# Seven quarter products in three sweeps instead of two, in the second MLP product of a decoder block

## The chip, the core and the metric

The kernel runs on one core of a Trainium2 chip. The engines are named as in the profile: PE (TensorE, matrix products; PEld is its weight load), DVE (VectorE), ACT (ScalarE), POOL (GpSimd) and SP (SyncE, which here only issues DMAs). PE writes to PSUM, which has 8 banks of 128 x 512 float32; all else works in SBUF, and data come from and go to DRAM by DMA. The metric is the device time of one execution in microseconds (us): 830.0 us, the median of three runs (829.31, 830.0 and 831.16).

## What is computed

One decoder layer on 512 tokens of width 1024 in float32: a mixer (attention, a gated convolution, a gated sum and a projection), then an MLP with 4096 features. The change touches the MLP's second product and what follows it:

```python
def squared_relu_mlp(h, w_ff1, w_ff2):
    return jnp.square(jax.nn.relu(h @ w_ff1)) @ w_ff2
...
f = squared_relu_mlp(rms_norm(x, norm_mlp_pre), w_ff1, w_ff2)
x = x + rms_norm(f, norm_mlp_post)
```

## The kernel before

**Split products.** Float32 accuracy is kept by writing each operand as a high part and a low part (`split`, L725: ACT casts the high part, DVE subtracts to get the low one), and by three matmuls for each product: high x high, high x low, low x high (`mm3`, L84 to 88). A matmul has 128 x 128 weights and moves 512 columns.

**First MLP product.** `h @ w_ff1` is done in 32 blocks j of 128 features. `wsplit` (L99) loads a block's weights in two pieces of 256 KB into buffers of tag raw (6 of them, L47), splits them into tags whi and wlo (4 each, L48), and `ff1_part` (L685) does 24 matmuls of 512 tokens into one PSUM bank. `ff1_end` (L694) squares the rectified result (ACT, then DVE at L699) into f1[j // 2]: a tile per pair p of blocks, holding features of both blocks (rows 0 and 1) for both token halves. The tiles of pairs 0 to 13 take all 14 buffers of tag w, the last two come from tag ra.

**Second MLP product as seven quarter products.** For a pair p, `f @ w_ff2` is a 2 x 2 block product: A has two token halves (256 tokens) and two feature rows, B two feature rows and two halves of 512 output columns. The Winograd form of Strassen's method replaces eight block products with seven, at the price of sums and differences of the quarters, which DVE forms. A block product is 6 matmuls (two token tiles x three), and its two banks accumulate over all 16 pairs.

- The first sweep is interleaved with the first product: after the blocks of pair p, `first_operands(p)` (L737) loads four quarters of w_ff2 (`quarter`, L720, tag raw), forms s23 and t3, t2, t4, and splits them; `first_sweep(p - 1)` (L757) issues the three block products of the pair before: P7 = s3 t3, P6 = s2 t2, P4 = a22 t4.
- The second sweep (L802 to 816) goes over the 16 pairs again. `second_operands(p)` (L762) loads the four quarters anew, forms t1, splits the f tile and the four right operands; `second_products` (L779) issues P1, P5, P2 and P3. The operands of pair 0 and product P1 of pair 0 stand ahead of the last first sweep.
- Between them (L807 to 812) e, g and h take up the sums of the first sweep, which frees its banks.
- The end (L834 to 854) does the products of the last two pairs (TAIL, L54) token tile by token tile. As each bank is complete, DVE combines it into o_, the output tiles. `post(t)` (L827) takes the squares' sums (ACT, and two small operations on POOL, L649 and L145), multiplies by the gain (L831), and `finish` (L820) scales, adds the residual x1 and stores (L824, L825). Token tiles t + 2 (lower half) and t (upper half) are finished in the same pass, t = 0 and then 1.

**What sets the order.** Each engine, and SP's queue of DMAs, works through its instructions in order. The order is not that of the source alone: a scheduler deals out instructions as their operands and buffers come free in its own model, earlier source lines first. A tile of a tag takes a buffer only when an earlier tile of that tag has been read for the last time. PSUM tags: ps (3 banks), sc (2), cv (2), tp (1). In the second MLP product further tags matter: h (hpool, 4 buffers; first-sweep operands, then the f tile's splits) and sw (r3, 4 buffers; right operands of the later sweeps).

Of the kernel before, what the change touches and what calls it, by code (L numbers as in the profile page):

```python
# [19 lines left out]
P = 128  # L20
# [38 lines left out]
def decoder_block(ctx: ExitStack, tc: tile.TileContext, a: dict, out: bass.AP):  # L59
# [676 lines left out]

    def first_operands(p):  # L737
# [17 lines left out]
        return (s3, s2, [a22[:, h] for h in half]), w  # L755
# [6 lines left out]
    def second_operands(p):  # L762

        b12, b11, b21, b22 = (quarter(2 * p + r, c, *t) for r, c, *t in (
            (0, 1, "whi", NSPLIT), (0, 0), (1, 0), (1, 1)))
        t1 = stage.tile([P, 512], F32, tag="wlo", name=f"t1{p}", bufs=NSPLIT)
        l = htile(f"l{p}")
        w = [r3.tile([P, 4, 512], F32R, tag="sw", name=f"y{x}{p}", bufs=4) for x in "hl"]
        split(l[:, 0:2, :], l[:, 2:4, :], f1[p])
        split(w[0][:, 0, :], w[1][:, 0, :], b11)  # L770
        dve.tensor_tensor(t1, b12, b11, ALU.subtract)
        for n, src in ((1, t1), (2, b21), (3, b22)):
            split(w[0][:, n, :], w[1][:, n, :], src)
        return l, w


    LEFT = ((0, 0), (0, 1), (1, 0), (1, 1))

    def second_products(p, ops, which, toks=(0, 1)):  # L779
        l, w = ops  # L780
        for n in which:
            r, c = LEFT[n]
            products(bcc[n], [l[:, r, half[c]], l[:, 2 + r, half[c]]], [x[:, n, :] for x in w], p == 0, p == NP - 1, toks)

    ops = {}
    for p in range(NP):
# [10 lines left out]
        if p == 1:  # L797
            acc = [[scs(f"p70"), scs("p71")], [cvtile("p60"), cvtile("p61")], [tps("p40"), ps("p41")]]
# [3 lines left out]
    second = second_operands(0)  # L802
    bcc = [[ps(f"p1{t}") for t in range(2)]]
    second_products(0, second, (0,))
    first_sweep(NP - 1, ops.pop(NP - 1))

    e, g = (ratile(n) for n in ("e", "g"))  # L807
    h = wtile("h")
    for t in range(2):
        act.copy(e[:, t, :], acc[1][t])  # L810
        dve.tensor_tensor(g[:, t, :], acc[0][t], e[:, t, :], ALU.add)
        dve.tensor_tensor(h[:, t, :], g[:, t, :], acc[2][t], ALU.subtract)
    bcc += [[cvtile(f"p5{t}") for t in range(2)], [scs(f"p2{t}") for t in range(2)], [tps("p30"), ps("p31")]]
    second_products(0, second, (1, 2, 3))
    for p in range(1, NP - TAIL):
        second_products(p, second_operands(p), range(4))
# [3 lines left out]
    def finish(t, r):  # L820
        for c, n in ((0, 512), (512, 512)) if t != 1 else ((0, 512), (512, 256), (768, 256)):
# [3 lines left out]
            sp.dma_start(out[t * P:(t + 1) * P, c:c + n], piece)  # L825

    def post(t):  # L827
        src = [o_[t][:, hf, :] for hf in range(2)]
        r = square_sums(src, f"o{t}")
        for hf in range(2):  # L830
            dve.tensor_tensor(src[hf], src[hf], gout[:, hf * 512:(hf + 1) * 512], ALU.mult)  # L831
        finish(t, r)

    last = [(p, second_operands(p)) for p in range(NP - TAIL, NP)]  # L834
    for t in range(2):
        v = stile(f"v{t}")
        for n in (0, 1, 2, 3):
            for p, x in last:
                second_products(p, x, (n,), (t,))
            bank = bcc[n][t]  # L840
            if n == 0:
                act.copy(v, bank)
                dve.tensor_tensor(o_[t + 2][:, 0, :], v, h[:, t, :], ALU.add)
            elif n == 1:
                dve.tensor_tensor(g[:, t, :], g[:, t, :], bank, ALU.add)
                dve.tensor_tensor(e[:, t, :], e[:, t, :], bank, ALU.add)  # L846
                dve.tensor_tensor(o_[t + 2][:, 1, :], g[:, t, :], v, ALU.add)
                post(t + 2)
                pool.tensor_tensor(e[:, t, :], e[:, t, :], v, ALU.add)  # L849
            elif n == 2:  # L850
                dve.tensor_tensor(o_[t][:, 0, :], v, bank, ALU.add)
            else:
                dve.tensor_tensor(o_[t][:, 1, :], e[:, t, :], bank, ALU.add)
                post(t)
# [61 lines left out]
```

## Time and profile before

| | us |
|---|---|
| median of three runs | 830.0 |
| the profiled execution | 830.19 |
| its span, first to last instruction | 828.4 |
| PE busy | 797.4 (96%) |
| DVE busy | 633.0 (76%) |
| ACT busy | 419.7 (51%) |
| POOL busy | 215.6 (26%) |

The table and all rows below are of the profiled execution. Times in rows count from the start of its span. A matmul's recorded duration is longer than the distance from one to the next, as matmuls are pipelined, so rates are read from starts. The granted PE clock is given as a share of full speed. An idle time in brackets ends with what released the engine; SPq marks DMA issues of SP, and a row that ends in "x2" merges two instructions.

### The profile page before, as it was taken

How to read it: one execution, taken by the hardware profiler on the slowest of the kernel's cores; microseconds unless marked ns; L12 is line 12 of the kernel's file. 1: busy time of each engine (PE TensorE's matmuls, PEld its weight loads, DVE VectorE, ACT ScalarE, POOL GpSimd, SP SyncE). 2: the span in 40 equal slices, each digit the busy share in tenths (PEclk: the TensorE clock that was granted, in tenths of full speed). 3: DMA queues.
4: the chain of work that ended last, by engine and by line, in shares of the span. 5: the costliest groups of instructions: out<-in, count | busy, mean ns of one | idle time of the engine just before them, and what ended most of it. 6: DMA issues, size and time to landing. Idle time of an engine off the chain costs nothing. (4 is left out here: it accounts for less than half of the span.)

```text
span 828.4 us, 11002 instructions
## 1 busy us (share of the span) xinstructions
PE 797.4 (96%) x3786; PEld 660.7 (80%) x3786; DVE 633.0 (76%) x1046; ACT 419.7 (51%) x792; POOL 215.6 (26%) x203
## 2 busy tenths in 40 slices
PE   8989999999999999899999999999999999999992
PEld 8967888888888887687878898888888888788871
DVE  5689999999999996596573547857657657798777
ACT  6667775867673233365442324434334334555642
POOL 3244433433434645648711100000000000000003
PEclk9999999999999999999999999999999999999997
DMA  8412121122112223245450014544434334466422
GB/s 265 137 41 90 52 80 51 53 80 70 68 62 100 91 101 104 89 162 188 159 191 1 27 49 155 178 135 144 141 127 153 128 127 165 154 210 202 157 67 101
DMA packets 54344, 96.36 MB, mean 116 GB/s; under 512 B 6288, under 2 KB 11280, under 8 KB 54288
## 3 DMA queue, kind: packets, MB, share of 16 engines
q1 hardware_dynamic: 53856, 94.09, 34.1%
q0 software_dynamic: 432, 1.57, 0.5%
q8 instruction: 30, 0.49, 0.3%
q14 instruction: 26, 0.21, 0.1%
HBM read 93.54 MB, written 2.10 MB: 115 GB/s over the span
## 5 line engine op out<-in xcount | busy, mean ns | idle before, releaser
L559 DVE SCALAR_TENSOR_TENSOR cv<-u,convw,cv 128x512 f32<-128x512 f32 x232 | 161.9, 747 | 0.2
L87 PE MATMUL pf<-h2l,whi_f 128*128 128x512 f32 (+1 forms) x256 | 97.4, 380 | 0.0
L86 PE MATMUL pf<-h2h,whi_f 128*128 128x512 f32 (+1 forms) x256 | 97.3, 380 | 0.0
L88 PE MATMUL pf<-h2h,wlo_f 128*128 128x512 f32 (+1 forms) x256 | 97.3, 381 | 0.0
L112 DVE TENSOR_TENSOR wlo_f<-raw_f,whi_f 128x512 fp32r<-128x512 f32 x60 | 41.1, 690 | 65.1 <-ACT whi_f L111 63.9
L849 POOL TENSOR_TENSOR e<-e,v 128x512 f32<-128x512 f32 x2 | 3.2, 1600 | 329.4 <-DVE e L846 329.4
L111 ACT CAST whi_f<-raw_f 128x512 fp32r<-128x512 f32 x60 | 36.9, 621 | 85.0 <-PE pf L87 50.0
L112 POOL TENSOR_TENSOR wlo_gt<-raw_gt,whi_gt 128x512 fp32r<-128x512 f32 x32 | 43.9, 1374 | 50.1 <-ACT whi_gt L111 50.1
L87 PEld LDWEIGHTS pf<-h2l,whi_f 128*128 128x128 f32 x256 | 48.2, 188 | 9.9
L86 PEld LDWEIGHTS pf<-h2h,whi_f 128*128 128x128 f32 x256 | 48.2, 188 | 9.9
L88 PEld LDWEIGHTS pf<-h2h,wlo_f 128*128 128x128 f32 x256 | 48.2, 188 | 9.8
L86 PE MATMUL pg<-hTh,whi_gt 128*128 128x512 f32 x128 | 51.4, 402 | 0.0
L88 PE MATMUL pg<-hTh,wlo_gt 128*128 128x512 f32 x128 | 50.6, 396 | 0.0
L87 PE MATMUL pg<-hTl,whi_gt 128*128 128x512 f32 x128 | 50.5, 395 | 0.0
L86 PE MATMUL p<-yh,l 128*128 128x512 f32 x128 | 50.4, 395 | 0.0
L87 PE MATMUL p<-yl,l 128*128 128x512 f32 x128 | 50.4, 395 | 0.0
L88 PE MATMUL p<-yh,l 128*128 128x512 f32 x128 | 50.2, 395 | 0.0
L726 ACT CAST yh<-f 128x512 fp32r<-128x512 f32 x48 | 28.0, 617 | 36.8 <-PE p L87 27.6
L727 DVE TENSOR_TENSOR yl<-f,yh 128x512 fp32r<-128x512 f32 x48 | 31.7, 687 | 14.8 <-ACT yh L726 14.7
L111 ACT CAST whi_gt<-raw_gt 128x512 fp32r<-128x512 f32 x32 | 19.8, 618 | 40.1 <-PE pg L87 37.0
L726 ACT CAST xh<-t 128x512 fp32r<-128x512 f32 x48 | 29.6, 619 | 19.5 <-DVE t L751 19.5
L727 DVE TENSOR_TENSOR xl<-t,xh 128x512 fp32r<-128x512 f32 x48 | 31.5, 684 | 0.5 <-ACT xh L726 0.5
(314 smaller groups left out, 2278.6 us busy)
## 6 DMA issues: line engine op xcount, KB each, us to landing
f<-in_w_ff SPq DMA_DIRECT2D x128, 256.0 KB, 3.0
raw_f<-in_w_ff SPq DMA_DIRECT2D x64, 256.0 KB, 3.0
raw_gt<-in_w_zm SPq DMA_DIRECT2D x32, 256.0 KB, 2.5
raw_gb<-in_w_zm SPq DMA_DIRECT2D x16, 256.0 KB, 2.6
raw_ga<-in_w_zm SPq DMA_DIRECT2D x16, 256.0 KB, 2.6
raw_wo<-in_w_o SPq DMA_DIRECT2D x16, 256.0 KB, 2.6
raw_pw<-in_w_pw SPq DMA_DIRECT2D x16, 256.0 KB, 2.7
raw_wout<-in_w_out SPq DMA_DIRECT2D x16, 256.0 KB, 2.7
```

The costliest lines, as they stand in the source:

```text
L86: pe.matmul(o, lhsT=lh, rhs=rh, start=first, stop=False)
L87: pe.matmul(o, lhsT=lh, rhs=rl, start=False, stop=False)
L88: return pe.matmul(o, lhsT=ll, rhs=rh, start=False, stop=last)
L111: recent[act] = act.copy(hi, raw)
L112: recent[e] = e.tensor_tensor(lo, raw, f32(hi), ALU.subtract)
L559: dve.scalar_tensor_tensor(co[j] if tap == CW - 1 else acc[j], src, convw[:, i, tap:tap + 1], acc[j], ALU.mult, ALU.add)
L726: act.copy(hi, src)
L727: dve.tensor_tensor(lo, src, f32(hi), ALU.subtract)
L849: pool.tensor_tensor(e[:, t, :], e[:, t, :], v, ALU.add)
```

## The change

The same seven products are dealt out as three, two and two. The first sweep now takes P1 = a11 b11, P6 = s2 t2 and P7 = s3 t3. In it DVE also forms t1 and t4, in the raw buffers of b12 and b21, and SP writes both to DRAM (`keep`, 2 x 256 KB per pair). The second sweep takes P5 and P4, for which t1 and t4 are read back (`later_operands(p, 0)`, two loads); with them the lower token half (tiles 2 and 3) is complete. The third sweep takes P2 and P3 with two quarters of w_ff2 (`later_operands(p, 1)`). During its first 14 pairs the generator `lower()` forms and finishes tiles 2 and 3, a step per pair. The last two pairs are again done tile by tile, now for tiles 0 and 1 only. The operands of pairs 0 and 1 of the second sweep, and P5 of both, stand ahead of the last first sweep. Matmuls per pair: 42, as before. Loads per pair: 8 quarter-sized DMAs, as before, and two writes.

```diff
+    dram = open_pool(ctx, "dram", bass.MemoryType.DRAM)
+    def keep(name, p, src):
+        kept[name, p] = dram.tile([P, 512], F32, tag=f"{name}{p}", name=f"{name}{p}")
+        sp.dma_start(kept[name, p], src)
     def first_operands(p):
...
-        a22 = stile(f"a22{p}", F32R)
-        split(a22[:, half[0]], a22[:, half[1]], f[:, 1, half[1]])
+        a11 = stile(f"a11{p}", F32R)
+        split(a11[:, half[0]], a11[:, half[1]], f[:, 0, half[0]])
+        split(w[0][:, 0, :], w[1][:, 0, :], b11)
...
-        ts = [stile(f"t{n}{p}") for n in (3, 2, 4)]
-        for n, (t, x, y, op) in enumerate(((ts[0], b22, b12, ALU.subtract), (ts[1], ts[0], b11, ALU.add), (ts[2], ts[1], b21, ALU.subtract))):
-            dve.tensor_tensor(t, x, y, op)
-            split(w[0][:, n, :], w[1][:, n, :], t)
-        dve.tensor_tensor(f[:, 1, half[1]], f[:, 1, half[0]], s23[:, half[0]], ALU.subtract)
+        t3, t2 = (stile(f"t{n}{p}") for n in (3, 2))
+        dve.tensor_tensor(t3, b22, b12, ALU.subtract)
+        dve.tensor_tensor(t2, t3, b11, ALU.add)
+        split(w[0][:, 2, :], w[1][:, 2, :], t3)
+        split(w[0][:, 1, :], w[1][:, 1, :], t2)
+        dve.tensor_tensor(b12, b12, b11, ALU.subtract)
+        keep("t1", p, b12)
+        dve.tensor_tensor(b21, t2, b21, ALU.subtract)
+        keep("t4", p, b21)
+        dve.tensor_tensor(f[:, 0, half[0]], f[:, 1, half[0]], s23[:, half[0]], ALU.subtract)
...
-    def second_operands(p):
-        b12, b11, b21, b22 = (quarter(2 * p + r, c, *t) for r, c, *t in (
-            (0, 1, "whi", NSPLIT), (0, 0), (1, 0), (1, 1)))
...
+    def later_operands(p, beta):
+        if beta:
+            raw = [quarter(2 * p + 1, c) for c in range(2)]
+        else:
+            raw = []
+            for n, (tag, bufs) in (("t1", ("whi", NSPLIT)), ("t4", ("raw", NRAW))):
+                raw.append(stage.tile([P, 512], F32, tag=tag, name=f"{n}b{p}", bufs=bufs))
+                sp.dma_start(raw[-1], kept[n, p])
+        l = hpool.tile([P, 4, 2 * P], F32R, tag="h", name=f"l{beta}{p}", bufs=4)
+        w = r3.tile([P, 4, 512], F32R, tag="sw", name=f"y{beta}{p}", bufs=4)
+        split(l[:, 0:2, :], l[:, 2:4, :], f1[p][:, :, half[1 - beta]])
+        for n in range(2):
+            split(w[:, n, :], w[:, 2 + n, :], raw[n])
         return l, w
...
-    e, g = (ratile(n) for n in ("e", "g"))
-    h = wtile("h")
+    u1, u2 = (ratile(n) for n in ("u1", "u2"))
+    u3 = wtile("u3")
     for t in range(2):
+        act.copy(u1[:, t, :], acc[0][t])
+    for t in range(2):
+        dve.tensor_tensor(u2[:, t, :], acc[1][t], u1[:, t, :], ALU.add)
+        dve.tensor_tensor(u3[:, t, :], acc[2][t], u2[:, t, :], ALU.add)
...
+    def lower():
+        for t in range(2):
+            yield from post(t + 2, (
+                lambda: dve.tensor_tensor(o_[t + 2][:, 0, :], u3[:, t, :], bcc[1][t], ALU.subtract),
+                lambda: dve.tensor_tensor(o_[t + 2][:, 1, :], u3[:, t, :], bcc[0][t], ALU.add),
+                lambda: dve.tensor_tensor(u2[:, t, :], u2[:, t, :], bcc[0][t], ALU.add)))
+    rest = lower()
+    for p in range(NP - TAIL):
+        later_products(p, 1, later_operands(p, 1))
+        next(rest, None)
+    last = [(p, later_operands(p, 1)) for p in range(NP - TAIL, NP)]
...
     for t in range(2):
-        v = stile(f"v{t}")
-        for n in (0, 1, 2, 3):
+        for n, src in ((0, u1), (1, u2)):
             for p, x in last:
-                second_products(p, x, (n,), (t,))
...
+                later_products(p, 1, x, (n,), (t,))
+            dve.tensor_tensor(o_[t][:, n, :], src[:, t, :], bcc[2 + n][t], ALU.add)
+        for _ in post(t, ()):
+            pass
```

`post` is now a generator: it does the combinations it is given, then what `post` and `finish` did, and yields after each DVE step (7 steps for a lower tile).

## Rows read from the trace of the kernel before

**Rows 1.** The page: busy time of each engine, share of the span.
```profile
PE 797.4 (96%) x3786; PEld 660.7 (80%) x3786; DVE 633.0 (76%) x1046; ACT 419.7 (51%) x792; POOL 215.6 (26%) x203
```

**Rows 2.** By stretch: length; busy of PE, PEld, DVE, ACT, POOL; clock; DMA; GB/s.
```profile
501.64:711.93 210.29, 210.29 (x910) 170.96 (x909) 138.48 (x253) 85.85 (x153) 0.00 (x0) 1.00 0.43 146
711.93:723.68 11.75, 9.77 (x43) 7.66 (x42) 10.19 (x18) 8.28 (x15) 0.00 (x0) 1.00 0.47 159
723.68:812.10 88.42, 88.42 (x379) 70.61 (x377) 73.44 (x104) 48.45 (x81) 3.02 (x4) 1.00 0.47 156
812.10:828.40 16.30, 0.00 (x0) 0.00 (x0) 11.57 (x18) 3.05 (x9) 5.18 (x7) 0.63 0.27 97
...
720.00:760.00 40.00, 40.00 (x173) 32.26 (x172) 36.95 (x52) 24.05 (x38) 0.00 (x0) 1.00 0.57 188
```

**Rows 3.** Timeline at the change of sweeps: start, duration, engine, line, operation.
```profile
711.53 0.40 PE L88 MATMUL pf<-h2h,wlo_f 128*128 128x512 f32 x1
715.65 0.40 PE L88 MATMUL p<-xh,a 128*128 128x512 f32 x1
718.03 0.73 PE L86 MATMUL p<-xh 128*128 128x512 f32 x2 [1.98 <-ACT xh L726]
...
708.95 0.62 ACT L726 CAST yh<-f 128x512 fp32r<-128x512 f32 x1 [1.96 <-PE pf L87]
712.02 0.60 ACT L696 ACTIVATE rl<-pf 128x512 f32<-128x512 f32 x1 [1.41 <-PE pf L88]
715.80 0.62 ACT L726 CAST yh<-f 128x512 fp32r<-128x512 f32 x1 [1.72 <-DMA f<-in_w_ff]
...
712.65 0.69 DVE L699 TENSOR_TENSOR f<-pf,rl 128x512 f32<-128x512 f32 x1 [1.15 <-ACT rl L696]
715.47 0.42 DVE L747 TENSOR_TENSOR s<-f 128x256 f32<-128x256 f32 x1
```

**Rows 4.** Timeline of the end, by engine.
```profile
811.70 0.40 PE L88 MATMUL p<-yh,l 128*128 128x512 f32 x1
...
803.71 0.69 DVE L843 TENSOR_TENSOR o<-v,h 128x512 f32<-128x512 f32 x1
806.11 1.79 DVE L831 TENSOR_TENSOR o<-o,g_out 128x512 f32<-128x512 f32 x1
820.62 0.67 DVE L853 TENSOR_TENSOR o<-e,p 128x512 f32<-128x512 f32 x1
823.67 1.54 DVE L824 SCALAR_TENSOR_TENSOR o<-o,r_o,x 128x512 f32<-128x512 f32 x3 [0.85 <-POOL r_o L145]
...
821.38 0.63 ACT L647 ACTIVATE j_o<-o 128x512 bf16<-128x512 f32 x1 [1.80 <-DVE o L853]
...
822.20 0.79 POOL L649 TENSOR_SCALAR v_o<-ss_o 128x1 f32<-128x1 f32 x1 [3.22 <-ACT j_o L647]
```

**Rows 5.** One pair of the first sweep: timeline, and its groups (idle last).
```profile
651.94 0.68 DVE L699 TENSOR_TENSOR f<-pf,rl 128x512 f32<-128x512 f32 x1
659.84 0.69 DVE L112 TENSOR_TENSOR wlo_f<-raw_f,whi_f 128x512 fp32r<-128x512 f32 x1 [1.32 <-ACT whi_f L111]
667.21 0.69 DVE L699 TENSOR_TENSOR f<-pf,rl 128x512 f32<-128x512 f32 x1
...
670.07 0.39 PE L86 MATMUL pf<-h2h,whi_f 128*128 128x512 f32 x1
...
670.13 1.26 SPq L104 DMA_DIRECT2D raw_f<-in_w_ff  x2
...
L112 DVE TENSOR_TENSOR wlo_f<-raw_f,whi_f 128x512 fp32r<-128x512 f32 x4 | 2.8, 692 | 5.4 <-ACT whi_f L111 5.4
```

**Rows 6.** Timeline of DVE, one pair of the second sweep: its first split and the next.
```profile
790.09 0.69 DVE L727 TENSOR_TENSOR yl<-f,yh 128x512 fp32r<-128x512 f32 x1 [1.26 <-ACT yh L726]
...
795.69 0.69 DVE L727 TENSOR_TENSOR yl<-f,yh 128x512 fp32r<-128x512 f32 x1 [1.26 <-ACT yh L726]
```

**Rows 7.** DMA issues of the output stores: KB each, median us to landing.
```profile
out<-o SPq DMA_DIRECT2D x7, 256.0 KB, 2.0
```

More of the change, by code (lines that the diff above doesn't have):

```diff
@@ L760, in first_sweep, with later_products @@
             products(bank, l, [x[:, n, :] for x in w], p == 0, p == NP - 1)
-    def second_operands(p):
-        b12, b11, b21, b22 = (quarter(2 * p + r, c, *t) for r, c, *t in (
-            (0, 1, "whi", NSPLIT), (0, 0), (1, 0), (1, 1)))
[L766 to L773, printed above, removed]
+    def later_operands(p, beta):
[11 more added lines that the diff above has]
+            split(w[:, n, :], w[:, 2 + n, :], raw[n])
         return l, w
-    LEFT = ((0, 0), (0, 1), (1, 0), (1, 1))
-    def second_products(p, ops, which, toks=(0, 1)):
+    def later_products(p, beta, ops, which=(0, 1), toks=(0, 1)):
         l, w = ops
         for n in which:
-            r, c = LEFT[n]
-            products(bcc[n], [l[:, r, half[c]], l[:, 2 + r, half[c]]], [x[:, n, :] for x in w], p == 0, p == NP - 1, toks)
+            r = 1 - n if beta else n
+            products(bcc[2 * beta + n], [l[:, r, :], l[:, 2 + r, :]], [w[:, n, :], w[:, 2 + n, :]],
+                     p == 0, p == NP - 1, toks)
     ops = {}
@@ L801, in decoder_block, with post @@
     gout = gain("g_out", a["norm_mlp_post"], D)
-    second = second_operands(0)
-    bcc = [[ps(f"p1{t}") for t in range(2)]]
-    second_products(0, second, (0,))
+    ahead = [later_operands(p, 0) for p in range(2)]
+    bcc = [[ps(f"p5{t}") for t in range(2)]]
+    for p in range(2):
+        later_products(p, 0, ahead[p], (0,))
     first_sweep(NP - 1, ops.pop(NP - 1))
-    e, g = (ratile(n) for n in ("e", "g"))
-    h = wtile("h")
+    u1, u2 = (ratile(n) for n in ("u1", "u2"))
+    u3 = wtile("u3")
     for t in range(2):
[L810 to L816, printed above, removed]
-    o_ = [wtile(f"o{t}") for t in range(NT)]
-    def finish(t, r):
+        act.copy(u1[:, t, :], acc[0][t])
+    for t in range(2):
+        dve.tensor_tensor(u2[:, t, :], acc[1][t], u1[:, t, :], ALU.add)
+        dve.tensor_tensor(u3[:, t, :], acc[2][t], u2[:, t, :], ALU.add)
+    bcc += [[f(f"{n}{t}") for t in range(2)] for f, n in ((scs, "p4"), (cvtile, "p2"))] + [[tps("p30"), ps("p31")]]
+    for p in range(2):
+        later_products(p, 0, ahead[p], (1,))
+    for p in range(2, NP):
+        later_products(p, 0, later_operands(p, 0))
+    o_ = [wtile(f"o{t}") for t in range(NT)]
+    def post(t, combine):
+        src = [o_[t][:, hf, :] for hf in range(2)]
+        for c in combine:
+            c()
+            yield
+        r = square_sums(src, f"o{t}")
+        for hf in range(2):
+            dve.tensor_tensor(src[hf], src[hf], gout[:, hf * 512:(hf + 1) * 512], ALU.mult)
+            yield
         for c, n in ((0, 512), (512, 512)) if t != 1 else ((0, 512), (512, 256), (768, 256)):
@@ L825, in finish @@
             sp.dma_start(out[t * P:(t + 1) * P, c:c + n], piece)
[L827 to L834, printed above, removed]
+            yield
+    def lower():
[9 more added lines that the diff above has]
+    last = [(p, later_operands(p, 1)) for p in range(NP - TAIL, NP)]
+    for _ in rest:
+        pass
     for t in range(2):
-        v = stile(f"v{t}")
-        for n in (0, 1, 2, 3):
+        for n, src in ((0, u1), (1, u2)):
             for p, x in last:
-                second_products(p, x, (n,), (t,))
[L840 to L854, printed above, removed]
+                later_products(p, 1, x, (n,), (t,))
+            dve.tensor_tensor(o_[t][:, n, :], src[:, t, :], bcc[2 + n][t], ALU.add)
+        for _ in post(t, ()):
+            pass
 def _layout(i):
```

5 lines of the change are left out of this document (3 added, 2 removed).

## Prediction

> **What bounds the kernel now.** I read the busy shares first: TensorE (PE) is busy 797.4 of 828.4 us [rows 1]. The table by stage says where the other 31 us are [rows 2]: PE is busy in every microsecond from 501.64 to 711.93 (first sweep) and from 723.68 to 812.10 (second sweep), misses 1.98 us in the stretch between them, and does nothing in the last 16.30 us, in which VectorE (DVE) still works 11.57 us. So in this half of the kernel a microsecond is to be had in two places only, the change of sweeps and the end. Everywhere else an edit must merely stay hidden behind PE.
>
> The change of sweeps, in the timeline [rows 3]: the 18 matmuls of the sweep for pair 14 end with the one at 715.65, the first for pair 15 starts at 718.03, after an idle 1.98 us that ended with ACT's cast of xh. ACT is in order. At 715.80 it first does a cast of second-sweep data (yh) that had waited 1.72 us for a DMA; the casts of xh stood behind it. The operands themselves were late too: every first-sweep product of pair 15 uses something made from f31, which is complete only at 712.65 + 0.69.
>
> The end [rows 4]: the last matmul starts at 811.70. From 803.71 to 825.21 DVE does the 29 operations that form and finish the four token tiles, at a pitch of about 0.60 us (a 0.69 us instruction overlaps the next a little), one L831 in each of the two passes stretched, as that at 806.11 (1.79 us). The chain that ended last is DVE's line almost throughout. The final link starts with the last combination (L853) at 820.62, 8.9 us after the last matmul; from there the square (821.38), POOL's two steps (from 822.20), three multiply-adds (823.67) and the output DMA take 828.40 - 820.62 = 7.78 us.
>
> **The change part by part.** *Matmuls.* Per pair 3 + 2 + 2 products instead of 3 + 4, each 6 matmuls: 42 per pair and 672 in all, as before, of the same shapes. At the rates seen, 15.27 us (651.94 to 667.21) for 66 matmuls (0.231 each) in the first sweep and 5.60 us for 24 (0.233) in the second [rows 5, 6], PE's work is unchanged: 0 us. The two later sweeps take 12 matmuls, 2.80 us, per pair.
>
> *First sweep, engines.* DVE gains one 128x512 operation per pair (t1 moves here; the split of b11 replaces the split of t4): 0.60 us against 5.4 us in which DVE idles per 15.27 us [rows 5]. ACT's casts are the same count. Cost 0; without that idle time it would be 16 x 0.60 = 9.6 us.
>
> *First sweep, the SP queue and the raw buffers.* Two 256 KB writes to DRAM per pair are new, each issued from SP in order after DVE's t1 and t4, and two of the six raw buffers (those of b12 and b21) stay taken until the write has landed. Behind them in SP's queue are the next loads, first the ff1 weights. The nearest row for a write is the output store: 2.0 us to landing [rows 7]. Now those loads start at 670.13, when t2 has freed b11 [rows 5]. In DVE's new order f (667.21, 0.60), four 256-wide steps (0.33 each), t3 and t2 precede t1, which ends at 670.9, or at 673.3 if four splits go first; with 0.33 us for the issue and 2.0 for the landing the buffer comes free at 673.2 to 675.6: the load is 3.1 to 5.5 us later. Its cover: the same load of the pair before has its low part finished at 659.84 + 0.69 = 660.53, and PE takes it up at 670.07 [rows 5], after the rest of ff1 and the sweep: 9.5 us. So 4.0 us are left at worst: cost 0. The bandwidth grows by 32 x 256 KB, 8.4 MB in 210 us, from 146 to about 186 GB/s; the second sweep's start moved 188 GB/s with PE busy in 40.00 of 40.00 us [rows 2].
>
> The Trainium skill (DMA: Bandwidth & Descriptors, Anatomy of one DMA) speaks against this part: a DMA's semaphore fires only when the last byte is confirmed in the target, and with HBM as target that can take surprisingly long. By its fit, an estimate for 256 KB is 2.0 + 0.6 = 2.6 us, 0.6 us over the store's row, and the sum would be the same. On that page alone the second rival below would get twice its chance; the row, a write to HBM too, speaks against it.
>
> *Change of sweeps.* Product 1 of a pair is now a11 x b11, which needs f30 and a raw quarter and not f31: 6 matmuls, 1.4 us of cover. s23 then has until 715.65 + 0.23 + 1.4 = 717.3, and its operations (f31 at 712.65 + 0.69 = 713.3, three of 0.33 to 0.42, cast 0.62, subtract 0.69) are done by 716 to 717. The second-sweep operands of pairs 0 and 1 use two 512-wide tiles and one buffer of tag sw each, which come free at 709 (the cast of yh at 708.95 had waited for PE) [rows 3]; their loads no longer wait for a third and fourth quarter. So of the 1.98 us nothing to all comes back; a late DRAM read can also make it worse. I take a remaining stall of 0.3 (gain 1.7), range 0 to 2.0, and keep more for a rival.
>
> *Second and third sweep.* Per pair three splits: 3 x 0.60 = 1.8 us of DVE and about 1.6 of ACT in 2.80 us. In the third sweep one further DVE operation of the lower half per pair, 14 steps in 14 pairs: 2.4 of 2.80 us, 86%; before it was 4.34 of 5.60, 78% (1.26 idle) [rows 6]. Loads stay at two quarters per 2.80 us, the 187 GB/s of now. PE covers it, with four operand tiles ahead: cost 0. One new dependency: u3 is a 15th tile of tag w, whose 14 buffers hold f0 to f26. It must wait until the third sweep's operands of pair 0 have read f0. Their h buffer is free three pairs, 8.4 us, before the third sweep; cast, subtract and u3's two adds take 2.5 us, and the banks that u3 empties are wanted 1.4 us into the sweep. Cover 7.3 us, cost 0.
>
> *The end.* Both lower tiles leave it, and with them POOL's L849. What remains is 6 operations for tile 0 and 7 for tile 1, and tile 0's can run while PE does tile 1's last 12 matmuls (2.8 us). The last combination thus starts after the last matmul instead of 8.9 us later. The lag from a matmul's start to the next engine's read of its bank is 0.49 us (711.53 to 712.02) [rows 3]. One or two operations of tile 0 may stand in front on DVE, 0 to 1.2 us; I take 0.3, since their scale from POOL comes at about the same moment. Then the chain of 7.78 us [rows 4], unchanged (its links are the same instructions in both).
>
> **The sum**, against this execution: last matmul at 811.70 - 1.98 + 0.3 = 810.0; + 0.49 + 0.3 = 810.8; + 7.78 = 818.6 us of span. This execution's time is 830.19, 1.79 over its span: 820.4 us. The median of the runs is 830.0, 0.2 below; I predict **820.3 us** (-9.7, 1.2%). Own range 818.3 (no stall, nothing in front, and a scatter of 1.4, about that of the three runs, 829.31 to 831.16) to 822.5.
>
> **The rivals.**
> 1. *Stall at a change of sweeps.* The pieces t1 and t4 come back from DRAM, or u3's buffer comes, later than PE wants them. For it: ACT and DVE are in order, one late load held back ACT for 1.72 us now, and three such places exist instead of one. Against: the operands of pairs 0 and 1 can be split from 709 on, and u3 has 7.3 us. It costs two or three such waits: 2 to 4 us more, 822.5 to 824.5.
> 2. *The writes hold the SP queue and the raw buffers.* This one ends slower. It decides where the ff1 load behind the writes comes more than 9.5 us later than now, that is 4.0 us beyond my worst case (each write landing in some 6 us rather than 2.0, or the loads queued behind both writes and the pair's next quarters). From there each excess microsecond counts 15 times; over 9.7 / 15 = 0.65 us of it the kernel is slower than before. With 1 to 1.5 us: 835 to 843. For it: SP is in order, and its loads already wait for DVE in each pair. Against: the 2.0 us row [rows 7], and 188 GB/s that held up nothing [rows 2].
> 3. *The lower half doesn't get done in the sweep.* If its steps pile up behind the operand splits, DVE's tail stays as it is, and only the stall is gained: 830.0 - 1.7 = 828.3. Against: 14 steps for 14 pairs, and 0.4 us free in each.
>
> **How the numbers follow.** Forecast 0.68, rival 1 0.16, rival 2 0.08, rival 3 0.05, and 0.03 for a small loss elsewhere that eats the gain. About 0.2% (1.7 us) is what a measurement can tell from no change here. Rival 3 lies on that line: 0.02 of it counts as faster, 0.03 as same. Faster: 0.68 + 0.16 + 0.02 = 0.86; same 0.03 + 0.02 (of the small losses) = 0.05; slower 0.08 + 0.01 = 0.09. The range reaches over rival 1: 818.3 to 824.5, which leaves out 0.16.
>
> **What would show it.** Right: PE busy without a gap from the first sweep to its end, last matmul at about 810; DVE with some 13 operations after 806, and 7.8 us from the last combination to the end; the new DRAM writes landing in about 2 us and ff1 casts still waiting for PE rather than for a DMA. Wrong: PE waiting for wlo_f or whi_f in the first sweep (rival 2), PE waiting between sweeps for a split of t1, t4 or for u3 (rival 1), or subtractions of u3 and out stores of rows 256 to 511 after the last matmul (rival 3).

## The result, and the profile after

The changed kernel takes **838.83 us** (median of four runs, 837.55 to 841.13), the kernel before 830.39 us beside it (four runs, 829.31 to 831.16): a ratio of 1.0106, 95% interval 1.008 to 1.0131. It is 8.4 us slower, and the forecast was 9.7 us faster.

The profiled execution took 838.5 us, with a span of 836.7. First the page, its busy line and three of its costliest groups (busy and mean ns of one, then the idle time ahead of them and what ended most of it):

```profile
PE 806.0 (96%) x3786; PEld 663.5 (79%) x3786; DVE 629.7 (75%) x1060; ACT 419.0 (50%) x806; POOL 211.3 (25%) x201
...
L88 PE MATMUL pf<-h2h,wlo_f 128*128 128x512 f32 (+1 forms) x256 | 98.7, 386 | 5.6 <-DVE wlo_f L112 5.4
...
L111 ACT CAST whi_f<-raw_f 128x512 fp32r<-128x512 f32 x60 | 36.9, 621 | 46.2 <-DMA raw_f<-in_w_ff 46.0
...
L726 ACT CAST xh<-f 128x512 fp32r<-128x512 f32 x16 | 9.9, 620 | 64.4 <-DMA f<-in_w_ff 63.6
```

PE now waits in the first MLP product for the low part of ff1 weights (L88 for wlo_f), which the prediction named as the sign of its second rival. Behind that stand ACT's casts, which wait for loads of the ff1 weights (46.0 us in all) and of a quarter (63.6).

Then the table by stage, as [rows 2]: from the first ff1 matmul to the last, on to the end of the change of sweeps, on to the last matmul, and the end. Columns: stretch, length, busy time of PE, PEld, DVE, ACT and POOL with their instructions, granted clock, DMA share, GB/s.

```profile
475.89:724.34 248.45, 241.99 (x1125) 196.12 (x1124) 158.65 (x289) 92.13 (x170) 2.33 (x5) 1.00 0.46 156
724.34:736.50 12.16, 9.24 (x34) 6.88 (x33) 10.20 (x20) 9.01 (x17) 0.00 (x0) 0.86 0.72 241
736.50:826.96 90.46, 90.46 (x389) 72.81 (x388) 70.66 (x114) 51.72 (x99) 3.52 (x6) 1.00 0.52 169
826.96:836.70 9.74, 0.40 (x2) 0.00 (x0) 5.08 (x9) 1.26 (x4) 1.47 (x3) 0.75 0.30 109
```

The same stretch of before, first to last ff1 matmul, is this row of the same view:

```profile
473.95:711.53 237.58, 237.58 (x1125) 197.56 (x1123) 152.77 (x278) 95.58 (x173) 2.33 (x5) 1.00 0.40 136
```

So the difference of the spans, 836.7 - 828.4 = 8.3 us, falls apart like this:

| stretch | before | after | difference |
|---|---|---|---|
| start of the span to the first ff1 matmul | 473.95 | 475.89 | +1.94 |
| to the last ff1 matmul (first sweep) | 237.58 | 248.45 | **+10.87** |
| to the last matmul of all | 100.17 | 102.62 | +2.45 |
| to the end | 16.70 | 9.74 | -6.96 |

The end gives most of what was forecast, and the first sweep takes more than that away. Its mean loss is 10.87 / 15 = 0.72 us per pair. The table by stage calls only 248.45 - 241.99 = 6.46 of the 10.87 us idle, because a matmul's recorded duration is longer than the distance to the next. Read from the starts, PE stops at 14 places, 13 of them for wlo_f, and the distances there are 10.3 us longer in all than at PE's pace.

The first row lies ahead of the sweeps, in code that the change leaves alone. About 1 us of its 1.94 us is PE's clock, which in after was lowered behind a gap near 53 us and in before was not (rows in the last section). The rest is several small shifts. In the runs below this stretch takes 475.15 to 478.75 us, and 475.52 to 476.64 in those that edit the kernel before (e5, e9, e10), so most of the 1.94 us is not the change's.

**One pair of the first sweep**, the counterpart of [rows 5]. First the timeline of SP's queue (start, duration, line; duration includes waiting inside a merged row), then DVE's and ACT's.

```profile
685.41 0.93 SPq L742 DMA_DIRECT2D t<-f  x2
686.39 1.53 SPq L722 DMA_DIRECT2D f<-in_w_ff  x3
687.97 0.90 SPq L104 DMA_DIRECT2D raw_f<-in_w_ff  x2
...
693.96 1.96 SPq L104 DMA_DIRECT2D raw_f<-in_w_ff  x2
...
701.94 0.93 SPq L742 DMA_DIRECT2D t<-f  x2
```

```profile
678.90 0.68 DVE L699 TENSOR_TENSOR f<-pf,rl 128x512 f32<-128x512 f32 x1
...
684.70 0.69 DVE L762 TENSOR_TENSOR f<-f,f 128x512 f32<-128x512 f32 x1
...
693.25 1.33 DVE L112 TENSOR_TENSOR wlo_f<-raw_f,whi_f 128x512 fp32r<-128x512 f32 x2 [1.07 <-ACT whi_f L111]
...
699.41 0.69 DVE L727 TENSOR_TENSOR xl<-t,xh 128x512 fp32r<-128x512 f32 x1 [1.70 <-ACT xh L726]
700.02 0.68 DVE L727 TENSOR_TENSOR xl<-s,xh 128x512 fp32r<-128x512 f32 x1
700.62 0.68 DVE L727 TENSOR_TENSOR xl<-t,xh 128x512 fp32r<-128x512 f32 x1
701.23 0.68 DVE L762 TENSOR_TENSOR f<-f,f 128x512 f32<-128x512 f32 x1
```

```profile
692.59 1.25 ACT L111 CAST whi_f<-raw_f 128x512 fp32r<-128x512 f32 x2 [1.14 <-DMA raw_f<-in_w_ff]
...
697.12 0.62 ACT L111 CAST whi_f<-raw_f 128x512 fp32r<-128x512 f32 x1 [2.48 <-DMA raw_f<-in_w_ff]
698.24 0.62 ACT L111 CAST whi_f<-raw_f 128x512 fp32r<-128x512 f32 x1 [0.50 <-DMA raw_f<-in_w_ff]
698.76 0.61 ACT L726 CAST xh<-t 128x512 fp32r<-128x512 f32 x1
```

Read the chain in order of time. The two writes of t1 and t4 are issued at 685.41. Behind them three quarters of the next pair are loaded (from 686.39), into buffers that b11 and the last two pieces of ff1 weights have just left. The four pieces of ff1 weights that a pair needs then go in two rounds through the two buffers of t1 and t4: two loads at 687.97, cast at 692.59, subtracted at 693.25, which frees the two buffers for the next two loads at 693.96, cast at 697.12 and 698.24. ACT is in order, so the casts of t3, s23 and t2 stand behind those two casts (698.76), DVE's three low parts behind them, t1 behind these (701.23), and the next writes at 701.94. That is a **closed loop** of 701.94 - 685.41 = 16.53 us, while PE's work for a pair is 15.27 [rows 5]. In the kernel before the quarters' buffers came free when t3, t2 and t4 were formed, right after f and ahead of most splits: the loads of 670.13 [rows 5] start 2.9 us after f's start, those of 687.97 here 687.97 - 678.90 = 9.1 us after it. There, too, the four pieces go in two rounds through two buffers (670.13 to 677.03), but 6.2 us earlier in the pair.

DVE is in order as well. The low parts of the second two pieces, whose casts end at 698.86, come only behind the three low parts, t1 and t4, and it is there that PE waits (a row of DVE, then one of PE):

```profile
702.77 1.28 DVE L112 TENSOR_TENSOR wlo_f<-raw_f,whi_f 128x512 fp32r<-128x512 f32 x2
...
703.50 0.50 PE L88 MATMUL pf<-h2h,wlo_f 128*128 128x512 f32 x1 [0.91 <-DVE wlo_f L112]
```

One thing more can be counted in this pair, from each load's issue to its tile's last reading or to the landing of its write: from 688.45 to 693.94 five raw tiles are alive (three quarters, two pieces), and not six as in the kernel before. The third piece waits for the buffer of the first while a sixth stands empty. So the loop is as long as it is by the order in which the scheduler dealt out the loads, and not by the number of buffers alone. Why it deals them so is not shown.

The waits of SP's queue in the first sweep (us in total, times, longest) carry the same reading: SP stands before the write of t1 up to 5.4 us, with all loads behind it, and then before the landing of ff1 weights whose buffers it needs again (the latter already 31.9 us in 15 waits, the longest 3.2, in the kernel before):

```profile
SPq L742 <- DVE f L762: 57.8, 15, 5.4
SPq L104 <- DMA raw_f<-in_w_ff: 48.3, 13, 4.9
```

The write itself is short, as this row of the DMA issues says (KB each, median us to landing), the counterpart of [rows 7]:

```profile
t<-f SPq DMA_DIRECT2D x32, 256.0 KB, 2.1
```

**The change of sweeps**, the counterpart of [rows 3]: timeline of PE, then of ACT, and the table by stretch right behind the gap.

```profile
724.34 0.40 PE L88 MATMUL pf<-h2h,wlo_f 128*128 128x512 f32 x1
724.57 0.39 PE L86 MATMUL p<-xh,a 128*128 128x512 f32 x1
...
728.45 0.40 PE L88 MATMUL p<-xh,xl 128*128 128x512 f32 x1
728.68 0.40 PE L86 MATMUL p<-xh,a 128*128 128x512 f32 x1
...
730.12 0.40 PE L88 MATMUL p<-xh,a 128*128 128x512 f32 x1
733.44 0.80 PE L86 MATMUL p<-y,l 128*128 128x512 f32 x1 [2.92 <-ACT l L726]
```

```profile
725.22 0.62 ACT L726 CAST y<-t1b 128x512 fp32r<-128x512 f32 x1 [1.26 <-DMA t1b<-t]
...
727.17 0.59 ACT L696 ACTIVATE rl<-pf 128x512 f32<-128x512 f32 x1
...
730.04 0.62 ACT L726 CAST y<-t1b 128x512 fp32r<-128x512 f32 x1 [0.94 <-DMA t1b<-t]
```

```profile
733.40:736.50 3.10, 3.06 (x8) 2.44 (x9) 3.10 (x7) 1.99 (x4) 0.00 (x0) 0.53 0.43 159
```

The gap of 1.98 us is gone from its place, and one of 2.92 us stands a little later, ahead of the second sweep's products (l is the split of an f tile). Behind it the granted clock is 0.53. ACT waits before it for pieces of t1 that are read back (t1b), and the rectifying of the last ff1 block stands behind the first of these waits: it starts 727.17 - 724.34 = 2.83 us after the start of that block's last matmul, against 0.49 in [rows 3].

**The end**, the counterpart of [rows 4], timeline by engine:

```profile
826.96 0.40 PE L88 MATMUL p<-y,l 128*128 128x512 f32 x1
827.20 1.41 DVE L849 SCALAR_TENSOR_TENSOR o<-o,r_o,x 128x512 f32<-128x512 f32 x2
...
828.52 0.68 DVE L871 TENSOR_TENSOR o<-u,p 128x512 f32<-128x512 f32 x1
...
831.53 1.54 DVE L849 SCALAR_TENSOR_TENSOR o<-o,r_o,x 128x512 f32<-128x512 f32 x3 [0.84 <-POOL r_o L145]
```

The last combination now stands 1.56 us behind the last matmul instead of 8.92.

### The profile page after: what moved, and what is told of

It reads as the page before. It is cut to its first block, busy times and chain, and to the rows that moved or that the text cites. A ratio compares the mean times of both kernels' runs of the same rounds, so it can differ in the third digit from the quotient of the medians.

```text
span 836.7 us, 11113 instructions
## 1 busy us (share of the span) xinstructions
PE 806.0 (96%) x3786; PEld 663.5 (79%) x3786; DVE 629.7 (75%) x1060; ACT 419.0 (50%) x806; POOL 211.3 (25%) x201
## 5 line engine op out<-in xcount | busy, mean ns | idle before, releaser
L88 PE MATMUL pf<-h2h,wlo_f 128*128 128x512 f32 (+1 forms) x256 | 98.7, 386 | 5.6 <-DVE wlo_f L112 5.4
L649 POOL TENSOR_SCALAR v_o<-ss_o 128x1 f32<-128x1 f32 x4 | 2.5, 614 | 345.1 <-ACT j_o L647 345.1
L88 PEld LDWEIGHTS pf<-h2h,wlo_f 128*128 128x128 f32 x256 | 48.1, 188 | 20.8 <-DVE wlo_f L112 11.3
L86 PE MATMUL p<-y,l 128*128 128x512 f32 x128 | 51.2, 400 | 2.9 <-ACT l L726 2.9
L87 PE MATMUL p<-y,l 128*128 128x512 f32 x128 | 51.0, 399 | 0.0
L88 PE MATMUL pg<-hTh,wlo_gt 128*128 128x512 f32 x128 | 50.6, 396 | 0.0
L88 PE MATMUL p<-y,l 128*128 128x512 f32 x128 | 50.4, 395 | 0.0
L727 DVE TENSOR_TENSOR xl<-f,xh 128x512 fp32r<-128x512 f32 x16 | 11.1, 692 | 51.6 <-ACT xh L726 51.6
L112 DVE TENSOR_TENSOR wlo_f<-raw_f,whi_f 128x512 fp32r<-128x512 f32 x60 | 39.4, 687 | 12.3 <-ACT whi_f L111 12.2
L726 ACT CAST xh<-f 128x512 fp32r<-128x512 f32 x16 | 9.9, 620 | 64.4 <-DMA f<-in_w_ff 63.6
L726 ACT CAST l<-f 128x512 fp32r<-128x512 f32 x32 | 19.7, 620 | 32.4 <-PE p L88 32.4
L696 ACT ACTIVATE rl<-pf 128x512 f32<-128x512 f32 x32 | 19.0, 595 | 32.2 <-PE pf L88 32.2
```

Of the source, the lines that this page charges most:

```text
L86: pe.matmul(o, lhsT=lh, rhs=rh, start=first, stop=False)
L87: pe.matmul(o, lhsT=lh, rhs=rl, start=False, stop=False)
L88: return pe.matmul(o, lhsT=ll, rhs=rh, start=False, stop=last)
L112: recent[e] = e.tensor_tensor(lo, raw, f32(hi), ALU.subtract)
L649: pool.tensor_scalar(v, ss[:, 0:1], ss[:, 1:2], EPS, ALU.add, ALU.add)
L696: act.activation(rl, pf, AF.Relu)
```

## The experiments

The table has all runs. Ratios are to the kernel before in the same comparison (its medians 831.35 beside e1 to e4, 831.98 beside e5 to e8, 832.58 beside e9 to e11); the four right columns are lengths of the same stretches as above, in the profiled execution, from the starts of matmuls in the timeline.

| run | median us | ratio, 95% interval | to first ff1 matmul | first sweep | to last matmul | end |
|---|---|---|---|---|---|---|
| before | 830.39 | | 473.95 | 237.58 | 100.17 | 16.70 |
| after | 838.83 | 1.0106 (1.008 to 1.0131) | 475.89 | 248.45 | 102.62 | 9.74 |
| e1 writes issued by POOL | 856.75 | 1.0293 (1.0251 to 1.0336) | 475.15 | 265.06 | 105.60 | 9.29 |
| e2 no writes | 837.33 | 1.0068 (1.0049 to 1.0088) | 475.26 | 245.76 | 105.94 | 9.34 |
| e3 b11 split later | 840.85 | 1.011 (1.0091 to 1.0129) | 475.68 | 254.87 | 100.15 | 9.30 |
| e4 no trip through DRAM | 824.27 | 0.9914 (0.9894 to 0.9933) | 476.36 | 237.60 | 99.61 | 9.33 |
| e5 before, late release | 847.95 | 1.0203 (1.0181 to 1.0224) | 476.64 | 246.83 | 103.83 | 16.70 |
| e6 no writes, t1 and t4 early | 826.64 | 0.994 (0.9921 to 0.9959) | 476.19 | 239.41 | 98.96 | 9.34 |
| e7 t1 and t4 early | 836.72 | 1.0064 (1.0039 to 1.0089) | 477.37 | 242.21 | 106.80 | 9.42 |
| e8 seventh buffer | 824.41 | 0.9912 (0.9893 to 0.9931) | 478.21 | 238.38 | 98.18 | 9.33 |
| e9 before, seventh buffer | 832.78 | 1.0012 (0.9996 to 1.0029) | 475.52 | 237.53 | 99.77 | 17.38 |
| e10 before, late release, seventh buffer | 836.24 | 1.0047 (1.0031 to 1.0062) | 476.17 | 241.73 | 101.22 | 17.38 |
| e11 seventh buffer, t1 and t4 early | 826.0 | 0.9911 (0.9892 to 0.993) | 478.75 | 238.44 | 97.94 | 9.27 |

The theory (R in the expectations): the raw buffers come back too late, because t1 and t4 overwrite two of them in place, behind the splits, and a write must then land. The rivals: the writes hold SP's queue (Q), the landing of the writes by itself, or ACT's in-order casts (A; that of the b11 quarter waits for its load ahead of everything else).

**e1: the writes from POOL's queue**, so that nothing in SP's queue stands behind them.

```diff
-        sp.dma_start(kept[name, p], src)
+        pool.dma_start(kept[name, p], src)
```

> The changed kernel, but the writes of t1 and t4 are issued by POOL, which is idle there; nothing waits behind them on SP any more. Three causes are open for the 12.8 us that the first sweep of the changed kernel is longer (its last ff1 matmul starts at 724.34 instead of 711.53). Theory Q (SP's order: the next pair's quarter loads stand behind the waiting writes): the sweep is back near 712 and the time falls by some 11 to 13 us, to 826 to 828. Theory R (the raw buffers are given back too late, whoever issues the writes): at most the 1 us of issue and wait per pair is saved where it counts, time within 3 us of 838.8. Theory A (ACT waits for the quarter b11, whose cast stands ahead of the casts of ff1 weights): no more than R, unless b11's load comes earlier, then as Q.

Measured: 856.75 us, which none of the three forecasts holds, and the first sweep is 16.6 us longer than that of after. The DMA issues and the waits of SP's queue say why (median landing; total, times, longest):

```profile
t<-f POOLq DMA_DIRECT2D x32, 256.0 KB, 3.8
```

```profile
SPq L104 <- DMA t<-f: 39.5, 25, 3.5
```

The writes' place in SP's queue is not the cause. The write issued by POOL lands in 3.8 us instead of 2.1, and 25 loads of ff1 weights now wait for a landing. 16.6 / 15 = 1.1 us more per pair for a write that is 1.7 us longer fits a write inside the loop.

**e2: no writes.** t1 and t4 are formed in place as in after, but nothing is stored; the second sweep loads plain quarters of w_ff2 in their stead, so P5 and P4 are other products.

```diff
     def keep(name, p, src):
-        sp.dma_start(kept[name, p], src)
+        pass
...
-                sp.dma_start(raw[-1], kept[n, p])
+                sp.dma_start(raw[-1], a["w_ff2"][2 * p + n][:, (1 - n) * 512:(2 - n) * 512])
```

> The changed kernel without the two writes to DRAM; the second sweep loads two raw quarters of w_ff2 in place of t1 and t4, so its products P5 and P4 are left wrong. All other operations stay, the sums t1 and t4 on DVE too. Q and R both: the first sweep loses most of its 12.8 us, time 826 to 829 (R: somewhat less gained, since t1 and t4 still hold b12, b11 and b21, 828 to 832). A: little changes, 835 to 839.

Measured: 837.33 us, first sweep 245.76. Of the 10.87 us only 2.69 go with the writes; 8.18 stay. The writes are not the main part. By the time alone this is theory A's forecast and misses that of R, which had put more on the writes; e3 tests A.

**e3: b11 split later**, behind the casts of a11, so that its cast doesn't hold up ACT.

```diff
-        split(a11[:, half[0]], a11[:, half[1]], f[:, 0, half[0]])
-        split(w[0][:, 0, :], w[1][:, 0, :], b11)
+        a_ = act.copy(a11[:, half[0]], f[:, 0, half[0]])
+        dve.tensor_tensor(a11[:, half[1]], f[:, 0, half[0]], f32(a11[:, half[0]]), ALU.subtract)
+        with tc.issue_after(a_.ins):
+            split(w[0][:, 0, :], w[1][:, 0, :], b11)
```

> The changed kernel with one order changed: the split of b11 is held on ACT behind the cast of a11, so behind the end of the pair's ff1 blocks, and no longer stands ahead of the casts of the next ff1 weights. A: the first sweep is back near 712, 826 to 829. Q and R: the loads behind the writes are as late as before, 836 to 839; a part of the gain (3 to 6 us) would say that ACT's wait is one link of the loop and not its cause.

Measured: 840.85 us, first sweep 254.87, 6.4 us longer than in after. The cast of b11 that waited for its load was no cause, but the 836 to 839 of the other two theories are missed as well. In a pair near 651 us the cast of b11 (650.78) and its low part (651.66) now stand ahead of t1 (656.58); how much of the 6.4 us that makes is not shown.

**e4: the same dealing into 3 + 2 + 2 products without the trip through DRAM.** The first sweep keeps P7, P6 and P4 as in the kernel before; the second takes P1 and P5 (b11 and b12 loaded anew, t1 formed there), the third P2 and P3. The combinations are adapted, and the lower half is again formed step by step.

```diff
+    def later_operands(p, r):
+        if r:
+            src = [quarter(2 * p + 1, c) for c in range(2)]
+        else:
+            b12, b11 = quarter(2 * p, 1, "whi", NSPLIT), quarter(2 * p, 0)
+            src = [b11, stage.tile([P, 512], F32, tag="wlo", name=f"t1{p}", bufs=NSPLIT)]
...
+        if not r:
+            dve.tensor_tensor(src[1], b12, b11, ALU.subtract)
```

> The kernel before with its second sweep cut in two, so that nothing needs to be kept: first sweep P7, P6, P4 as before; second P1 and P5 (loads b11 and b12, t1 formed on DVE); third P2 and P3. The lower half is again complete after the second sweep and is formed and finished step by step in the third. All three theories: no writes, so the first sweep ends as in the kernel before (last ff1 matmul about 711.5), the change of sweeps costs 1 to 3 us as in the two kernels, and the end gains what the changed kernel's end gained (7 us): 822 to 825, faster than both. If the end gains less because DVE has 2.4 to 3.0 of 2.8 us to do per pair in the third sweep, 825 to 830.

Measured: 824.27 us, faster than both kernels. The first sweep is that of before to 0.02 us, the end is 7.37 us shorter, and a gap of 1.49 us stays at the change of sweeps. What the change was after can be had. In after it is lost in the first sweep and at the change of sweeps right behind it.

**e5: the kernel before with late release.** b12 and b21 are overwritten once more after the splits, which are two further DVE operations per pair; no writes, no other dealing of the products.

```diff
-            split(w[0][:, n, :], w[1][:, n, :], t)
+            act.copy(w[0][:, n, :], t)
+            lo_ = dve.tensor_tensor(w[1][:, n, :], t, f32(w[0][:, n, :]), ALU.subtract)
+        dve.tensor_tensor(b12, b12, b11, ALU.subtract)
+        dve.tensor_tensor(b21, ts[1], b21, ALU.subtract)
```

> The kernel before with one thing of the changed first sweep alone: after the pair's splits DVE overwrites b12 with b12 - b11 and b21 with t2 - b21 (the results aren't used), so that b12, b11 and b21 stay in their raw buffers until the end of the pair's DVE work, as in the changed kernel; no write, no split of b11, two sweeps. The runs so far leave the writes 2.7 us of the 10.9 us by which the first sweep grew (10.9 with them, 8.2 without). Theory R (the raw buffers come back too late for the next ff1 loads): most of those 8.2 us appear here, 836 to 840. Rival B (it is the split of b11, a fourth user of that quarter, or the order that it gives ACT): 830 to 832, only 1.2 us more DVE work per pair, hidden.

Measured: 847.95 us, 2.0% slower and more than the 840 of R's forecast; first sweep +9.25 us and +3.66 to the last matmul. SP's queue waits for the first of the two late operations (L754, the loads of quarters):

```profile
SPq L722 <- DVE f L754: 73.6, 14, 7.0
```

The late return of the raw buffers (of b11 too, which L754 reads) is enough for a loss of this size, in a kernel without writes; e10 below has the same operations and one buffer more.

**e6 and e7: t1 and t4 right after t2, ahead of all splits**, in e6 without the writes (as e2), in e7 with them.

```diff
-        split(w[0][:, 3, :], w[1][:, 3, :], s23)
...
-        split(w[0][:, 2, :], w[1][:, 2, :], t3)
-        split(w[0][:, 1, :], w[1][:, 1, :], t2)
         dve.tensor_tensor(b12, b12, b11, ALU.subtract)
         keep("t1", p, b12)
-        dve.tensor_tensor(b21, t2, b21, ALU.subtract)
+        t4_ = dve.tensor_tensor(b21, t2, b21, ALU.subtract)
         keep("t4", p, b21)
+        with tc.issue_after(t4_.ins):
+            split(w[0][:, 3, :], w[1][:, 3, :], s23)
+            split(w[0][:, 2, :], w[1][:, 2, :], t3)
+            split(w[0][:, 1, :], w[1][:, 1, :], t2)
```

> The changed kernel without writes (P5 and P4 are left wrong, as before) and with t1 and t4 formed right after t2, ahead of the three low-part subtractions, so that b12 and b21 come back some 2 us earlier in each pair. R: the first sweep loses most of its 8.2 us, time 827 to 832. B: as without writes alone, 836 to 838.

> The changed kernel with its writes, and t1 and t4 formed right after t2, ahead of the low-part subtractions. R: the raw buffers come back 2 us earlier per pair and SP waits less for the writes' data; the write's landing (2.1 us) still holds two of them, so half to most of the 10.9 us go, 828 to 834. B: 836 to 839.

Measured: 826.64 and 836.72 us. The first is just below R's forecast, the second misses it and lies in B's, although its first sweep gained as R said. With after and e2 this makes a table of two by two for the first sweep's loss against before: late with writes 10.87, late without 8.18, early with writes 4.63, early without 1.83. The place on DVE costs 6.2 to 6.4 us, the writes 2.7 to 2.8, whichever is taken first. The two add up, as parts of one delay would, the time after which the buffers return. e7 loses the rest at the change of sweeps, where gaps of 4.1 and 1.1 us stand.

**e8: a seventh buffer.** The changed kernel with b12 loaded into the ninth buffer of another tag (u), of which the residual x1 holds eight at this stage. No instruction of the first sweep is left out.

```diff
-        b12, b22, b11, b21 = (quarter(2 * p + r, c) for r, c in ((0, 1), (1, 1), (0, 0), (1, 0)))
+        b12, b22, b11, b21 = (quarter(2 * p + r, c, *t) for r, c, *t in ((0, 1, "u"), (1, 1), (0, 0), (1, 0)))
```

> The changed kernel with its writes and its order of operations, and a seventh buffer for what the six raw buffers hold: quarter b12 (which becomes t1) is loaded into the one spare buffer of tag u. R: the ff1 loads get a third buffer in the first sweep and no longer wait for the pair's end; the first sweep is back within 3 us of the kernel before, 826 to 832. If SP's order (loads behind the writes) is as much a cause, it stays above 834. B: 836 to 839.

Measured: 824.41 us, 14.4 us below after's median (16.0 with each set against its own runs of before) and below R's 826 to 832. The table by stage, and the timeline of SP around the writes of a pair:

```profile
478.21:716.59 238.38, 238.38 (x1125) 197.09 (x1123) 161.66 (x293) 95.55 (x174) 2.35 (x5) 1.00 0.52 167
716.59:728.75 12.16, 11.95 (x51) 9.29 (x50) 11.27 (x22) 6.74 (x13) 0.00 (x0) 1.00 0.73 226
```

```profile
689.38 0.33 SPq L104 DMA_DIRECT2D raw_f<-in_w_ff  x1
693.06 0.93 SPq L745 DMA_DIRECT2D t<-f  x2
694.03 1.50 SPq L104 DMA_DIRECT2D raw_f<-in_w_ff  x2
695.63 0.38 SPq L725 DMA_DIRECT2D f<-in_w_ff  x1
696.10 0.38 SPq L104 DMA_DIRECT2D raw_f<-in_w_ff  x1
```

PE is busy without a gap through the first sweep, with the writes and with t1 and t4 behind the splits, and the gap at the change of sweeps is 0.2 us. So the late return of the buffers is the cause, shown from the other side. What e8 does not separate is the number of buffers from the order of the loads: with the seventh buffer the scheduler puts one piece of ff1 weights ahead of the writes and the other three right behind them, where after has three quarters first. No run has the new order without the buffer.

**e9, e10, e11: controls for the seventh buffer**: the kernel before with it, e5 with it, and e7 with it (the edits are those above, taken together).

> The kernel before, with b12 loaded into a seventh buffer (the ninth of tag u, which stands empty in this stage) and nothing else changed. Control for the two runs beside it. If the raw buffers were no limit in the kernel before (its PE is busy without a gap there), this is 829 to 833 us. If they cost something already, it is faster than before by over 2 us.

> The kernel before with the late overwriting of b12 and b21 that made it 847.95 us, and b12 in the seventh buffer. The loop through the raw buffers explains the whole loss: 829 to 834 us, first ff1 matmul to last ff1 matmul 237.6 to 239 us. If instead the two further DVE operations per pair, or the splits done in another order, cost the time: 840 to 848 us.

> The changed kernel with b12 in the seventh buffer and with t1 and t4 (and their writes) formed right after t2, ahead of the splits. If the buffers' return was all that held the first sweep, it is bought already with the seventh buffer, and this is 823 to 826 us, as that run (824.41). If DVE's order costs or brings something by itself: below 822 or above 827 us.

Measured: 832.78, 836.24 and 826.0 us. By itself the buffer brings nothing (ratio 1.0012, interval 0.9996 to 1.0029): before, six were enough. In e10 it takes back 12.3 of e5's 16.0 us (each against its own runs of before); the period from f to f is 18.4 and 16.6 us in two of the first pairs and 15.3 (PE's pace) in eight that follow, so the loop no longer sets the pace. Of the 241.73 - 237.58 = 4.15 us that stay in the first sweep, 3.7 are one stop of PE for a low part, by the starts from 543.33 on, with the lowered clock behind it (its row is in the last section):

```profile
543.33 0.50 PE L88 MATMUL pf<-h2h,wlo_f 128*128 128x512 f32 x1 [1.81 <-DVE wlo_f L112]
```

That misses the 829 to 834 expected of it. With the buffer, DVE's order doesn't matter: e11 has the first sweep of e8 to 0.06 us.

## Why the prediction was wrong

**What bounds the kernel: right.** PE without gaps is the floor, and a microsecond was to be had only in two places. With the loop relieved, PE is busy for 238.38 of 238.38 us in the first sweep (e8).

**Matmuls, DVE's and ACT's work in the first sweep: right.** 3786 matmuls in both; e8 has all of the added DVE work (161.66 against 152.77 us busy) and its first sweep is 0.80 us longer than before.

**The step that failed: "The SP queue and the raw buffers ... cost 0".** Its parts were nearly right. The writes land in 2.1 us against the 2.0 taken, so the Trainium skill's warning (DMA: Bandwidth & Descriptors, Anatomy of one DMA: with HBM as target the receipt can take surprisingly long) is not borne out by this row. The fit that the prediction took from the same section stands there for DMAs issued by GpSimd, and on that path the write took 3.8 us (e1) and not 2.6. t1's place was near its late end: in the pair shown it is done 684.70 + 0.69 - 678.90 = 6.5 us after f, against 6.1 in the bound. Not ff1 weights but three quarters came first behind the writes, and so the load is 9.1 - 2.9 = 6.2 us later in the pair, against 5.5 at worst. That is still less than the 9.5 us of cover, and PE waited all the same. What was wrong is the comparison. The lateness of one load was set against the 9.5 us that the low part stood ready in the trace of before, as if each pair began with that stock anew. But the load's lateness comes back to its own cause: the casts of late ff1 weights stand in ACT's queue ahead of the casts of t3, s23 and t2, and the low parts of the last ones stand in DVE's behind t1 and t4, so t1 and the buffers of the next pair are later still, until the stock is used up and the loop's own length sets the pace. The number to form was the length of the loop over the two free buffers, two rounds of load, cast and subtraction, then three casts, three subtractions, t1, write, to be held against 15.27. It is 16.53 in the pair shown; on average 15.27 + 0.72 = 16.0 (from the write of t1 at 526.64 to that at 701.94, eleven pairs later, it is 15.94).

**Rival 2: right in place, wrong in its trigger, and right in size by luck.** It was given 835 to 843 us, which holds the 838.83, but for an excess of 1 to 1.5 us per pair. With the 0.72 that were measured its own sum is 820.3 + 15 x 0.72 = 831; the other 7 us came from elsewhere (the balance below). And it was to decide only from writes of some 6 us, or from loads queued behind both writes and the pair's next quarters. The writes took 2.1 us. The ff1 loads did stand behind both writes and three quarters, though the issues from 685.41 to 687.97 are only 2.6 us; what counted was that the delay comes back in each pair. A chance of 0.08 was far too low for a resource of which three of six (b12, b11 and b21) were to be held longer.

**The change of sweeps: right where nothing was late, wrong in after.** Behind the last ff1 matmul (724.34) come the 18 matmuls of pair 14, and product 1 of pair 15 follows these at once (728.45, 728.68) and covers its 1.4 us, as forecast. Then 2.92 us of gap and the lowered clock come, where 0.3 was taken: the stretch to the last matmul lost 2.45 us instead of gaining 1.7. That was rival 1, with ACT waiting for t1 as it is read back, but as a follow-on of the late buffers: the first of these loads is issued 724.34 - 720.34 = 4.0 us ahead of the last ff1 matmul, and with the seventh buffer 716.59 - 704.72 = 11.9 us ahead of it; there the gap is 0.2 us (e8), and the stretch gains 1.99. The loss does not grow with the lateness, though: in e3, whose first sweep is longer still, the stretch is 100.15, as before.

**Second and third sweep: right.** PE is busy in 90.46 of 90.46 us, and no row has it wait for u3.

**The end: right in kind, 1.2 us short.** From the last matmul to the end 9.74 us against 0.49 + 0.3 + 7.78 = 8.57. In front of the last combination stood two multiply-adds of tile 0 (1.41 us) rather than half of one: 828.52 - 826.96 - 0.49 = 1.07 instead of 0.3, inside the bound of 1.2. The chain behind it is 836.70 - 828.52 = 8.18 instead of 7.78; the difference lies after the last multiply-adds begin (836.70 - 831.53 = 5.17 against 828.40 - 823.67 = 4.73), where now two stores of tile 0 stand ahead in SP's queue; that these cause it was not tested.

**The balance.** Misses against the forecast in the profiled execution: 10.87 for the first sweep, 2.45 + 1.68 = 4.13 for the change of sweeps, 1.17 for the end, 1.94 ahead of the changed part: 18.1 us, from 820.4 to 838.5. In e8 the three changed stretches sum to +0.80 - 1.99 - 7.37 = -8.56 us, against -1.68 - 8.13 = -9.81 by the forecast's terms. So with the late buffers out of the way the other terms of the sum are sound to 1.3 us. Of the 18.1 us, 10.87 are the failed step and 4.13 came along with it; the 1.17 of the end and the 1.94 ahead of the sweeps have nothing to do with it.

**Best versions found:** e4, e8 and e11, all 0.9% faster than the kernel before, with intervals that lie over each other.

## What to carry to other kernels

When an edit holds a buffer longer, don't set the delay against the slack seen in the old trace: follow the buffer round, from its release through the load, the casts and whatever stands behind those in order, back to its next release, and hold that length against the period of the bound engine. Overwriting a staging buffer in place to save space, and doing it at the end of a step, is a late release even if the operation takes 0.6 us. Here a spare buffer of another tag brought more than a reordering (824.41 us in e8, 836.72 in e7), and it changed the order of the loads with it: look at the order that was dealt, and count the buffers that are in use, before adding one. If the operand that must be kept can instead be formed in a later sweep from quarters that are loaded there anyway, the trip through DRAM isn't needed at all (e4).

## What the runs showed of the hardware

**PE's clock after a gap.** The length of a gap does not decide by itself whether the granted clock falls. In the same unchanged code near 53 us, a gap of 2.26 us (before) was followed by the full clock and one of 2.25 us (after) by the lower of the two levels. A gap of 1.81 us (e10) was followed by the lower level, one of 3.22 us (e1) by the full one. These are the rows behind these four gaps, in this order, of the table by stretch (columns as above):

```profile
53.64:57.05 3.41, 3.01 (x17) 2.23 (x16) 2.00 (x3) 3.38 (x7) 2.58 (x10) 1.00 0.08 14
53.64:57.05 3.41, 3.41 (x13) 2.91 (x12) 1.83 (x3) 3.00 (x7) 2.98 (x10) 0.50 0.00 0
544.68:548.09 3.41, 3.41 (x10) 2.63 (x9) 0.69 (x1) 0.62 (x1) 0.00 (x0) 0.50 0.64 208
648.79:652.79 4.00, 4.00 (x17) 3.29 (x18) 1.15 (x2) 0.00 (x0) 0.00 (x0) 1.00 0.88 283
```

At the change of sweeps the clock stayed at 1.00 behind 1.98 us (before) and 1.49 us (e4), and fell behind 1.75 us (e10), 2.92 us (after) and 4.1 us (e7). What else decides is not shown by these runs. In after the lower clock takes (1 - 0.53) x 3.10 = 1.5 us more behind the gap of 2.92. With e8's 98.18 us, which has 0.2 of gap, that gives 98.18 - 0.2 + 2.92 + 1.5 = 102.4 of the 102.62 measured. So the lower clock made this gap half as dear again.

**Writes issued by POOL** land in 3.8 us, those issued by SP in 2.1, for the same 256 KB from the same buffers. The Trainium skill (DMA: Bandwidth & Descriptors, Specifications) gives a first-byte latency of some 1 us for GpSimd's path and 0.6 for SyncE's, a difference of 0.4; here the landings differ by 1.7, at the rates of this stage.
